# Sums of x on VectorE behind the keys, a smaller rotary table ahead of V's weights, one buffer set for key parts, output gates in the convolution's buffers

## The chip, the cores and the metric

The kernel runs on one core of one Trainium2 chip. The metric is the device time of one execution in microseconds (us). The engines are TensorE (PE, matrix products), VectorE (DVE), ScalarE (ACT), GpSimd (POOL) and the queue of SyncE (SP), which issues most transfers. Each engine works through its own list of instructions in order; an instruction whose data are not there holds everything behind it on that engine.

## The reference

One layer of a streaming encoder on 1024 prompt tokens and 64 sample tokens (1088 columns), width 1024:

```python
qa, ka, va, za, qkv_b, a_b, b_b, z_b, g_a, g_b = in_projection(x, w_in)
qa, ka = partial_rope(qa, pos), partial_rope(ka, pos)        # first 16 of 64 dims
y_a = (window_attention(qa, ka, va, sinks) * silu(za)) @ w_o_attn
qb, kb, vb = split(silu(causal_conv(qkv_b)))
y_b = (gated_rmsnorm(gated_delta_chunked(l2norm(qb), l2norm(kb), vb, g, beta)) * silu(z_b)) @ w_o_delta
h = sigmoid(g_a) * y_a + sigmoid(g_b) * y_b
y = layer_norm(ALPHA * x + h @ w_out)
```

Here g = -exp(a_log) * softplus(a_b + dt_bias) and beta = sigmoid(b_b). The partial rotary turns 16 of the 64 dimensions of each head; the other 48 stay as they are. New keys, values, convolution rows and states are outputs too.

## The kernel before, in words

All matrix products are made with operands split in a high and a low part (`split`: ACT copies the high part, DVE subtracts it to get the low part), and three products hi*hi, hi*lo, lo*hi are summed in PSUM. x lies transposed in eight tiles `ring` of 1088 columns, its raw form in `self.raw` (tiles `ring2`, shown as `ring` in the profile too).

The order of the first 165 us is: load and split x (`load_x`); project the keys for two pairs of heads in three column groups of 384, 384 and 320 (`branch_a_keys`, banks `bg`); project V and the decay inputs a, b for nine token tiles (`vab`, banks `pj`, with `wx` and `wt` as weights); project two tiles of z (`early`, banks `pj`, of which there are three), with two small groups of products of the decay (`gates`, banks `bg`) woven between; then `stream`, a Strassen-like scheme of seven products per pair of weight tiles, which needs sums and differences of blocks of x (`sums_x`) and of the weights (`weights7`).

A key group goes: ACT copies the bank to `rraw`; DVE rotates it (`rope`: a shuffle, two products with the table `cs`, an addition); ACT and DVE split it in `khi` and `klo`, of which there are two buffers each; SP writes both to DRAM (`k_d`). The sample's cached keys `ck` go the same way behind them. V's tile is evacuated by ACT (`V` at L448 and `abt` at L449). The ninth tile is added by DVE (L452). The first product of `gates` (`bg<-abt,u`) needs this `abt`; the second group (`bg<-scr,...`) needs a chain over DVE and ACT that ends with the product at L503.

```python
self.mm(sw[:, :144], swap, abt...)              # gates, after 24 products of early
nc.vector.tensor_copy(g4[...], sw[...])          # L488, L489
nc.vector.tensor_tensor(a, gbr, dtb, ALU.add)    # L495, then ACT: Abs, Exp, Ln
nc.vector.tensor_tensor(g, g, ea, ALU.mult)      # L503, then the four products
```

The sums of x are 16 subtractions of 128 x 544 values on GpSimd. They are read only from `split_sums` on, which runs with the second half of `early`.

Far later `out_a` (about 1060 to 1206 us) projects branch A's output in eight tiles; each column group is evacuated by one DVE instruction (L1134) that multiplies the bank with a gate loaded from DRAM (`gA_d`) into one of four buffers `gt`, and stored to `hA_d`. Its first tile runs while DVE works on the block inverse of branch B (L915, L917).

The code is written per stage; a list scheduler with priorities (`urgent`, `weave`) sets the order on each engine except where `keep_in_program_order` pins it. All matrix products are pinned.

Of the kernel before, what the change touches and what calls it, by code (L numbers as in the profile page):

```python
# [12 lines left out]
F32R = mybir.dt.float32r  # L13
# [3 lines left out]
ALU = mybir.AluOpType  # L17
# [7 lines left out]
NT = SEQ + DEC  # L25
# [13 lines left out]
HN = NT // 4  # L39
QUARTERS = tuple((i * HN, HN) for i in range(4))  # L40
SWAPMASK = [i + 8 if i % 16 < 8 else i - 8 for i in range(32)]
KSWAPMASK = [i + 8 if i < 8 else i - 8 if i < 16 else i for i in range(32)]
HS = (slice(0, 64), slice(64, 128))
# [12 lines left out]
class Build:  # L56
# [210 lines left out]

    def sums_x(self):
        halves = lambda k: [self.raw[k].rearrange("p (g h n) -> p h g n", g=2, h=2)[:, h] for h in range(2)]
        sub = lambda d, x, y: self.nc.gpsimd.tensor_tensor(d, x, y, ALU.subtract)  # L270
        self.late, self.mid = [], []
        with self.urgent():
            for k in range(4):
                (b11, b12), (b21, b22) = halves(k), halves(4 + k)
                t4 = self.t(self.vb, [128, 2, HN], "t4", bufs=4)
                sub(b11, b12, b11)
                t3 = self.t(self.vb, [128, 2, HN], "t3") if k == 3 else b12
                sub(t3, b22, b12)
                sub(b22, b22, b11)
                sub(t4, b21, b22)  # L280
                self.late.append(t4)
                self.mid.append(t3)
# [133 lines left out]
    def vab(self):  # L416
        nc, I = self.nc, self.I
        wt = []
        for k in (0, 4):
            wr = self.t(self.wp, [128, 4, 272], "wraw", bufs=2)  # L420
            parts = [self.t(pool, [128, 4, 272], tag, F32R, bufs=b)
                     for pool, tag, b in (((self.ws, "wx", 3), (self.ws, "wx", 3)) if k == 0 else ((self.ws, "wx", 3), (self.vb, "wt", 1)))]
            with self.urgent():
                nc.sync.dma_start(wr, I["w_vab"][k : k + 4].rearrange("k p c -> p k c"))
                self.split(*parts, wr)
            wt.append(parts)
        hi, lo = ([wt[kt // 4][s][:, kt % 4] for kt in range(KT)] for s in range(2))
        self.V = self.t(self.ap, [128, 9, 256], "V")
        abt = self.t(self.ap, [128, 9, 16], "abt")
        with self.urgent():  # L430
            rest = self.rest(self.t(self.wp, [128, KT, 128], "whi", F32R, bufs=2), self.ring)
        self.sums_x()
        nc.vector.memset(abt, 0.0)
        for t in range(9):
            m = 128 if t < 8 else 64
            ps = self.pjt()
            o = ps[:m, :272]
            for kt in range(KT):
                if t < 8:
                    xh, xl = (self.ring[kt][:, s, t * 128 : t * 128 + m] for s in (0, 1))  # L440
                    self.mm(o, xh, hi[kt], kt == 0, False)
                    self.mm(o, xl, hi[kt], False, False)
                    self.mm(o, xh, lo[kt], False, kt == KT - 1)
                else:
                    self.mm(ps[:, :272], rest[:, kt], hi[kt], kt == 0, False)
                    self.mm(ps[:, :272], rest[:, kt], lo[kt], False, kt == KT - 1)
            with self.urgent():
                nc.scalar.activation(self.V[:m, t, :], ps[:m, :256], AF.Copy)  # L448
                nc.scalar.activation(abt[:m, t, :], ps[:m, 256:272], AF.Copy)  # L449
        with self.urgent():  # L450
            for dst, c in ((self.V, slice(0, 256)), (abt, slice(256, 272))):
                nc.vector.tensor_tensor(dst[:m, 8, :], ps[64:128, c], dst[:m, 8, :], ALU.add)  # L452
        return abt
# [71 lines left out]
            nc.vector.tensor_copy(self.egs[HS[h]], self.egc[HS[1 - h]])  # L525


    def rope(self, raw, sh, a, n, swap):
        nc = self.nc
        nc.vector.stream_shuffle(sh, raw, swap)  # L530
        nc.vector.tensor_tensor(raw, raw, self.cosT[:, a : a + n], ALU.mult)
        nc.vector.tensor_tensor(sh, sh, self.sinT[:, a : a + n], ALU.mult)

    def load_rope(self, pool, name):
        cs = self.t(pool, [128, 2, NT], "cs")
# [2 lines left out]

    def branch_a_keys(self):
        nc, I = self.nc, self.I  # L540
        self.load_rope(self.vb, "rope")
        self.ck = self.t(self.vb, [128, 2, 128], "ck")
        nc.sync.dma_start(self.ck, I["cache_k"])


        def put(gp, src, dst):
            n = src.shape[-1]
            for s, part in enumerate(self.key_parts(src)):
                for hf in range(2):
                    nc.sync.dma_start(self.k_d[gp, :, 2 * s + hf, dst : dst + n], part[HS[hf]].bitcast(F32))  # L550

        for g, (a, n) in enumerate(GROUPS):
            for gp in range(2):
                ps = self.ps()[:, :n]
                for kt in range(KT):
                    self.drain(self.mm3(ps, *self.w0[gp], kt, a, n, kt == 0, kt == KT - 1))
                raw, sh = (self.t(self.vb, [128, 384], x, bufs=2)[:, :n] for x in ("rraw", "rsh"))
                nc.scalar.activation(raw, ps, AF.Copy)
                self.rope(raw, sh, a, n, KSWAPMASK)
                nc.vector.tensor_tensor(raw, raw, sh, ALU.add)  # L560
                w = min(n, SEQ - a)
                put(gp, raw[:, :w], a)
                if g == 2:
                    put(gp, raw[:, w:], SEQ + 128)
                    nc.sync.dma_start(self.O["o_nkp"][:, gp], raw[:, w - 128 : w])
                    nc.sync.dma_start(self.O["o_nks"][:, gp, 64:128], raw[:, w:])
        ck = self.ck
        for gp in range(2):
            put(gp, ck[:, gp], SEQ)
        nc.sync.dma_start(self.O["o_nks"][:, :, 0:64], ck[:, :, 64:128])  # L570

    def key_parts(self, src):
        n = src.shape[-1]
        parts = [self.t(self.vb, [128, 384], x, F32R, bufs=2)[:, :n] for x in ("khi", "klo")]
        self.split(*parts, src)
        return parts

# [9 lines left out]
    def front(self):  # L587
        nc = self.nc
        self.done = False

        def query(j):
            held = {}

            def ev(m, a, ps, add):
                g, h = divmod(a // HN, 2)
                first = (m, g) not in held
                if first:
                    held[m, g] = self.t(self.rq, [128, 2, 2 * HN], "qsp", F32R, bufs=4)
                q = held[m, g]
                parts = [q[:, s, h * HN : (h + 1) * HN] for s in range(2)]  # L600
                if j > 0 and add is None:
                    with self.urgent():
                        self.split(*parts, ps)
                else:
                    raw = self.t(self.rq, [128, HN], "rraw", bufs=4)
                    self.land(raw, ps, add)
                    if j == 0:
                        sh = self.t(self.rq, [128, HN], "rsh", bufs=2)
                        self.rope(raw, sh, a, HN, SWAPMASK)
                        nc.vector.tensor_tensor(raw, raw, sh, ALU.add)  # L610
                    self.split(*parts, raw)
                if not first:
                    for s in range(2):
                        dst = self.qd[s, 128 * j : 128 * j + 128].rearrange("p (c m i) -> p c m i", m=2, i=CH)[:, :, m]
                        w, c = q[:, s].bitcast(F32), 0 if g == 0 else 32
                        nc.sync.dma_start(dst[:, 9 * g : 9 * g + 8], w[:, c : c + 512].rearrange("p (c i) -> p c i", i=CH))
                        nc.sync.dma_start(dst[:, 8, c : c + 32], w[:, 512 - 16 * c : 544 - 16 * c])
            return ev
# [509 lines left out]
    def out_a(self, w):  # L1128
        nc = self.nc
        for t in range(8):  # L1130
            def ev(g, a, n, ps):
                tg = self.t(self.mp, [128, 384], "gt", bufs=4)
                (nc.sync if t else nc.scalar).dma_start(tg[:, :n], self.gA[t, :, a : a + n])
                nc.vector.scalar_tensor_tensor(tg[:, :n], tg[:, :n], 1.0, ps, ALU.add, ALU.mult)  # L1134
                nc.sync.dma_start(self.hA[t, :, a : a + n], tg[:, :n])
            yield from self.project(ev, edge=t in (0, 7), w=None if t else w)
# [213 lines left out]
def tables():  # L1350
# [30 lines left out]
    b = p // 16 % 2  # L1381
    masks = np.stack([f((b == 1) & (j < 16)), f((b == 0) & (j >= 16))], axis=1)
    return rope, ropeq, cf, cg, masks


# [63 lines left out]
```

## Time and profile before

| | before |
|---|---|
| median of 3 runs | 1410.66 us (1408.94 to 1410.67) |
| the profiled execution | 1408.06 us, span 1406.3 us |
| PE busy | 1364.9 us (97%) |
| DVE, ACT, POOL busy | 989.3 (70%), 624.0 (44%), 231.8 us (16%) |
| mean granted TensorE clock | 0.995 |

The span runs from the first to the last instruction; 1.8 us lie around it. Each row of a timeline has the start, the length and the instruction, then in brackets how long the engine stood idle before it and what ended the wait. A row of the waits names who waited for whom, the total, how often, and the longest.

### The profile page before, as it was taken

What the parts mean: (1) busy time and instruction counts of PE and PEld (TensorE: products, weight loads), DVE (VectorE), ACT (ScalarE), POOL (GpSimd) and SP (SyncE); (2) the same over time, 40 slices, a digit from 0 to 9 for tenths busy, and PEclk for the clock granted to TensorE, in tenths of its full rate; (3) what the DMA queues carried; (4) which work ended last, traced back from release to release, by engine and by line L of the source; (5) the groups of instructions that cost most, each with busy time, mean ns of one, the idle gap of its engine ahead of it and who ended that gap; (6) DMA issues with size and microseconds to landing.
All of it is one profiled execution on the core that took longest, in us unless ns stands there. A gap on an engine that the chain in (4) does not pass through costs nothing. (4 is left out here: it accounts for less than half of the span.)

```text
span 1406.3 us, 30878 instructions
## 1 busy us (share of the span) xinstructions
PE 1364.9 (97%) x11850; PEld 1270.8 (90%) x11850; DVE 989.3 (70%) x2404; ACT 624.0 (44%) x1764; POOL 231.8 (16%) x379
## 2 busy tenths in 40 slices
PE   8889999999999999999999999999998999999997
PEld 7889999999989899988999889988998889999886
DVE  8668555877777568867796777867788555655675
ACT  5263444555555444356633665256642443422000
POOL 4323223111111023111221113021220100000000
PEclk9999999999999999999999999999999999999998
DMA  7425566666665420210321003210346225564221
GB/s 241 117 79 131 144 135 183 190 183 180 170 183 165 123 87 31 73 36 17 93 80 57 32 24 100 82 57 17 124 137 226 73 74 167 192 219 137 95 94 71
DMA packets 152500, 162.47 MB, mean 116 GB/s; under 512 B 54304, under 2 KB 135840, under 8 KB 151968
## 3 DMA queue, kind: packets, MB, share of 16 engines
q1 hardware_dynamic: 138368, 148.59, 35.4%
q10 hardware_dynamic: 13632, 10.78, 2.5%
q8 instruction: 94, 1.54, 0.5%
q0 software_dynamic: 352, 1.11, 0.2%
q14 instruction: 54, 0.44, 0.1%
HBM read 111.74 MB, written 48.70 MB: 114 GB/s over the span
## 5 line engine op out<-in xcount | busy, mean ns | idle before, releaser
L108 PE MATMUL pj<-ring,whi 128*128 128x384 f32 (+2 forms) x2856 | 678.3, 327 | 5.8 <-DVE gt L1134 4.0
L108 PEld LDWEIGHTS pj<-ring,whi 128*128 128x128 f32 x2856 | 480.1, 189 | 17.2 <-issue 13.3
L108 PE MATMUL pj<-ring,wlo 128*128 128x384 f32 (+2 forms) x1680 | 466.2, 321 | 0.9 <-DVE rsh L471 0.8
L108 PEld LDWEIGHTS pj<-ring,wlo 128*128 128x128 f32 x1680 | 288.4, 188 | 5.8 <-issue 4.1
L812 DVE SCALAR_TENSOR_TENSOR acc<-pre,sm,acc 128x384 f32<-128x384 f32 (+1 forms) x216 | 134.0, 627 | 24.2 <-ACT acc L810 20.7
L108 PE MATMUL pj<-ring,wx 128*128 128x272 f32 x756 | 109.7, 291 | 2.9 <-ACT u L365 2.8
L88 ACT ACTIVATE whi<-wraw 128x1024 fp32r<-128x1024 f32 (+2 forms) x72 | 66.7, 927 | 82.4 <-PE pj L108 48.8
L108 PEld LDWEIGHTS pj<-ring,wx 128*128 128x128 f32 x756 | 99.6, 188 | 3.8 <-ACT u L365 3.8
L91 DVE TENSOR_TENSOR wlo<-wraw,whi 128x1024 fp32r<-128x1024 f32 (+2 forms) x58 | 68.0, 1172 | 40.4 <-ACT whi L88 35.3
L108 PE MATMUL bg<-ring,whi 128*128 128x384 f32 (+2 forms) x408 | 84.5, 317 | 5.6 <-ACT ring L88 5.2
L108 PEld LDWEIGHTS bg<-ring,whi 128*128 128x128 f32 x408 | 65.6, 190 | 7.0 <-ACT ring L88 5.2
L108 PE MATMUL pj<-pl,ring 128*128 128x512 f32 (+1 forms) x240 | 70.1, 375 | 0.0
L704 ACT ACTIVATE P<-bg,nm 128x192 f32<-128x192 f32 (+2 forms) x136 | 54.4, 408 | 33.4 <-DVE nm L697 32.1
L1024 DVE SCALAR_TENSOR_TENSOR S<-S,dec,bg 128x128 f32<-128x128 f32 x128 | 38.7, 344 | 39.2 <-PE bg L108 38.3
L813 ACT ACTIVATE gt<-acc 128x384 f32<-128x384 f32 (+1 forms) x72 | 36.4, 505 | 62.3 <-DVE acc L812 62.0
L108 PE MATMUL bg<-ring,wlo 128*128 128x272 f32 (+2 forms) x288 | 63.5, 307 | 0.0
L1002 ACT ACTIVATE qs<-bg,egs 64x128 f32<-64x128 f32 x128 | 46.4, 362 | 29.1 <-DVE R L999 27.4
L999 DVE SCALAR_TENSOR_TENSOR R<-bg,negc,t2k 64x128 f32<-64x128 f32 x128 | 44.6, 348 | 16.1 <-PE bg L108 14.9
L336 POOL TENSOR_TENSOR sums<-wraw 128x512 f32<-128x512 f32 x14 | 18.3, 1308 | 220.4 <-DMA wraw<-w_tiles 109.4
L819 DVE SCALAR_TENSOR_TENSOR plb<-gt,acc 128x384 f32<-128x384 f32 (+1 forms) x96 | 43.1, 461 | 15.6 <-ACT gt L813 15.3
L108 PEld LDWEIGHTS pj<-pl,ring 128*128 128x128 f32 x240 | 44.1, 188 | 8.2
L810 ACT ACTIVATE acc<-pre,sm 128x384 f32<-128x384 f32 (+1 forms) x72 | 42.8, 597 | 15.6 <-DVE plb L819 5.9
(277 smaller groups left out, 2317.3 us busy)
## 6 DMA issues: line engine op xcount, KB each, us to landing
wraw<-w_tiles SPq DMA_DIRECT2D x80, 512.0 KB, 3.9
q_d<-qsp SPq DMA_DIRECT2D x32, 256.0 KB, 3.5
keys<-k_d SPq DMA_DIRECT2D x28, 256.0 KB, 4.2
q<-q_d SPq DMA_DIRECT2D x64, 96.0 KB, 2.7
gA_d<-gs SPq DMA_DIRECT2D x32, 136.0 KB, 2.2
plb<-prodA SPq DMA_DIRECT2D x8, 544.0 KB, 4.4
plb<-prodB SPq DMA_DIRECT2D x8, 544.0 KB, 5.1
z<-zA_d SPq DMA_DIRECT2D x16, 256.0 KB, 3.2
```

What stands on the lines that cost most here:

```text
L88: i = self.nc.scalar.activation(hi, raw, AF.Copy)
L91: self.nc.vector.tensor_tensor(lo, raw, hi.bitcast(F32), ALU.subtract)
L108: self.tc.keep_in_program_order(self.nc.tensor.matmul(o, l, r, start=start, stop=stop, skip_group_check=skip))
L336: sub = lambda d, x, y, op: nc.gpsimd.tensor_tensor(d, x, y, op)
L704: nc.scalar.activation(P[:, hf, k], ps[:, k], AF.Exp, bias=nm[:, hf, b : b + 1], scale=0.125, accum_out=sm[:, hf, b : b + 1])
L810: nc.scalar.activation(acc[:, :w], pre[:, 0:w], AF.Copy, scale=cw(0))
L812: nc.vector.scalar_tensor_tensor(acc[:, :w], pre[:, j : j + w], cw(j), acc[:, :w], ALU.mult, ALU.add)
L813: nc.scalar.activation(th[:, :w], acc[:, :w], AF.Tanh, scale=0.5)
L819: nc.vector.scalar_tensor_tensor(o, v(th), 1.0, v(acc), ALU.add, ALU.mult)
L999: nc.vector.scalar_tensor_tensor(R[HS[h]], ks[HS[h], col[h]], self.negc[HS[h], p, c : c + 1], e["vs"][HS[h], i], ALU.mult, ALU.add)
L1002: nc.scalar.activation(qs[HS[1 - h]], ks[HS[1 - h], col[h]], AF.Copy, scale=self.egs[HS[1 - h], p, c : c + 1])
L1024: nc.vector.scalar_tensor_tensor(Sn[:, h], S[:, h], self.egl[h][:, p, c : c + 1], kv[:, 0:128], ALU.mult, ALU.add)
```

## The change

1. `sums_x` runs on VectorE instead of GpSimd, pinned in program order, and is called after the rotation of the last key group instead of ahead of V's products.
2. The rotary table of the keys is written by two memsets on GpSimd (1 and 0), and only its 2 x 16 rows that differ are loaded, ahead of V's weights, instead of the 1088 KB table behind the weights of `early`.
3. The key parts and the four sums `t4` share one set of seven buffers `parts`, instead of two `khi`, two `klo` and four `t4`. The cached keys' parts now stand behind the sums.
4. The rotation's four instructions on DVE are pinned in order, for the keys.
5. In `out_a` the gates are loaded into the convolution's buffers `acc` and `pre` (two each) and, for the third column group from tile 1 on, into `gt`.

```diff
 def sums_x(self):
-        sub = lambda d, x, y: self.nc.gpsimd.tensor_tensor(d, x, y, ALU.subtract)
+        sub = lambda d, x, y: self.tc.keep_in_program_order(self.nc.vector.tensor_tensor(d, x, y, ALU.subtract))
...
-                t4 = self.t(self.vb, [128, 2, HN], "t4", bufs=4)
+                t4 = self.t(self.vb, [128, 2 * HN], "parts", bufs=7).rearrange("p (g n) -> p g n", g=2)
 def vab(self):
-        self.sums_x()
 def rope(...):
+        keep(nc.vector.tensor_tensor(raw, raw, sh, ALU.add))
 def branch_a_keys(self):
-        self.load_rope(self.vb, "rope")
+        cs = self.t(self.vb, [128, 2, NT], "cs")
+        nc.gpsimd.memset(cs[:, 0], 1.0)
+        nc.gpsimd.memset(cs[:, 1], 0.0)
+        with self.urgent():
+            for h in HS:
+                rows = slice(h.start, h.start + 16)
+                nc.sync.dma_start(cs[rows], I["rope"][rows])
...
+        self.sums_x()
         ck = self.ck
 def key_parts(self, src):
-        parts = [self.t(self.vb, [128, 384], x, F32R, bufs=2)[:, :n] for x in ("khi", "klo")]
+        parts = [self.t(self.vb, [128, 2 * HN], "parts", F32R, bufs=7)[:, :n] for _ in range(2)]
 def out_a(self, w):
-                tg = self.t(self.mp, [128, 384], "gt", bufs=4)
+                tg = (self.t(self.mp, [128, 384], "gt", bufs=4) if t and g == 2 else
+                      self.t(self.bp, [128, (384, 390)[g % 2]], ("acc", "pre")[g % 2], bufs=2))
```

PE's order is the same in both kernels, instruction by instruction. Three places on the engines that it waits for are shown.

ACT, around the evacuation of V's last three tiles. Before, the splits of the last key group and of both halves of the cached keys (`ck`) stand between these evacuations:

```order
L448 ACTIVATE V_521<-pj_689 128x256
L449 ACTIVATE abt_522<-pj_689 128x16
L88 ACTIVATE khi_482<-rraw_467 128x64
L448 ACTIVATE V_521<-pj_716 128x256
L449 ACTIVATE abt_522<-pj_716 128x16
L88 ACTIVATE khi_492<-ck_230 128x128
L88 ACTIVATE khi_500<-ck_230 128x128
L448 ACTIVATE V_521<-pj_743 128x256
L449 ACTIVATE abt_522<-pj_743 128x16
L448 ACTIVATE V_521<-pj_770 64x256
L449 ACTIVATE abt_522<-pj_770 64x16
```

The changed kernel has at the same place (its `parts` are the former `khi`; lines count about one less here):

```order
L88 ACTIVATE parts_477<-rraw_470 128x256
L88 ACTIVATE parts_485<-rraw_470 128x64
L447 ACTIVATE V_545<-pj_719 128x256
L448 ACTIVATE abt_546<-pj_719 128x16
L447 ACTIVATE V_545<-pj_746 128x256
L448 ACTIVATE abt_546<-pj_746 128x16
L447 ACTIVATE V_545<-pj_773 64x256
L448 ACTIVATE abt_546<-pj_773 64x16
L88 ACTIVATE whi_935<-wraw_934 128x1024
L469 ACTIVATE rraw_848<-pj_800 128x384
L88 ACTIVATE parts_516<-ck_233 128x128
L88 ACTIVATE parts_524<-ck_233 128x128
```

The two splits of `ck` have moved behind the ninth tile and behind the tanh of the first z group.

DVE, between the ninth tile's addition and the chain of `gates`. Before:

```order
L452 TENSOR_TENSOR V_521<-pj_770,V_521 64x256
L452 TENSOR_TENSOR abt_522<-pj_770,abt_522 64x16
L487 COPY scr_824<-abt_522 64x9x8
L91 TENSOR_TENSOR wlo_933<-wraw_931,whi_932 128x1024
L488 COPY scr_824<-bg_822 64x9x8
L489 COPY scr_824<-bg_822 64x9x8
L471 SCALAR_TENSOR_TENSOR rraw_845<-rraw_845,pj_797 128x384
L495 TENSOR_TENSOR scr_824<-scr_824,sm_219 128x68
```

The changed kernel, from behind the same addition of `abt` on:

```order
L270 TENSOR_TENSOR ring_7_102<-ring_7_102,ring_3_98 128x2x272
L91 TENSOR_TENSOR wlo_936<-wraw_934,whi_935 128x1024
L270 TENSOR_TENSOR parts_505<-ring_7_102 128x544
L270 TENSOR_TENSOR ring_4_99<-ring_4_99 128x2x272
L270 TENSOR_TENSOR t_73_512<-ring_8_103,ring_4_99 128x544
L470 SCALAR_TENSOR_TENSOR rraw_848<-rraw_848,pj_800 128x384
L270 TENSOR_TENSOR ring_8_103<-ring_8_103,ring_4_99 128x2x272
L486 COPY scr_827<-abt_546 64x9x8
L487 COPY scr_827<-bg_825 64x9x8
L270 TENSOR_TENSOR parts_510<-ring_8_103 128x544
L91 TENSOR_TENSOR parts_517<-ck_233,parts_516 128x128
L488 COPY scr_827<-bg_825 64x9x8
```

Six of the sixteen sums (L270) stand between the addition of `abt` and the last copy out of `bg`; the other ten stand ahead of it, behind the last key's parts.

On ACT again, the stretch from the decay's exponentials to the second z group. Before, two splits of the stream's weights (`wx`) stand ahead of that group's tanh (L470):

```order
L507 ACTIVATE beta_841<-scr_824 128x68
L496 ACTIVATE scr_824<-scr_824 128x68
L497 ACTIVATE scr_824<-scr_824 128x68
L498 ACT_TABLE_LOAD
L498 ACTIVATE scr_824<-scr_824 128x68
L88 ACTIVATE wx_1080<-sums_1069 128x512
L88 ACTIVATE wx_1089<-wraw_1067 128x512
L470 ACT_TABLE_LOAD
L470 ACTIVATE rsh_889<-pj_849 128x384
```

The changed kernel:

```order
L506 ACTIVATE beta_844<-scr_827 128x68
L469 ACTIVATE rsh_892<-pj_852 128x384
L495 ACTIVATE scr_827<-scr_827 128x68
L496 ACTIVATE scr_827<-scr_827 128x68
L497 ACT_TABLE_LOAD
L497 ACTIVATE scr_827<-scr_827 128x68
L88 ACTIVATE ghi_840<-scr_827 128x68
L517 ACT_TABLE_LOAD
L517 ACTIVATE dec_882<-bg_877 128x272
```

The tanh has moved ahead of the exponentials, and the two `wx` splits have left this place; they stand some ten instructions later.

## Rows read from the trace of the kernel before

**Rows 1.** The page's busy times: us, share of the span, instructions.

```profile
PE 1364.9 (97%) x11850; PEld 1270.8 (90%) x11850; DVE 989.3 (70%) x2404; ACT 624.0 (44%) x1764; POOL 231.8 (16%) x379
```

**Rows 2.** PE's waits over the span: total us, times, longest.

```profile
PE pj L108 <- DVE gt L1134: 4.0, 1, 4.0
...
PE pj L108 <- DVE rsh L471: 2.0, 2, 1.2
...
PE pj L108 <- DVE rraw L471: 0.6, 1, 0.6
```

**Rows 3.** PE's timeline from the end of the keys to the stream.

```profile
32.38 1.92 PE L108 MATMUL pj<-wx,ring 128*128 128x272 f32 x14
...
35.38 1.93 PE L108 MATMUL pj<-wx,ring 128*128 128x272 f32 x14
...
45.36 2.33 PE L108 MATMUL pj<-wx,ring 128*128 128x272 f32 x14 [3.78 <-ACT abt L449]
...
62.62 1.30 PE L108 MATMUL pj<-wx,whi 128*128 128x272 f32 x9
...
64.62 0.51 PE L108 MATMUL pj<-ring,whi 128*128 128x384 f32 x2
...
71.30 0.48 PE L108 MATMUL bg<-abt,u 128*128 128x144 f32 x2 [2.35 <-ACT rraw L470]
...
76.45 0.44 PE L108 MATMUL bg<-scr,u 128*128 128x68 f32 x2 [0.50 <-DVE scr L503]
...
103.27 1.76 PE L108 MATMUL pj<-ring,wx 128*128 128x272 f32 x12 [0.86 <-ACT u L365]
...
117.04 1.79 PE L108 MATMUL pj<-ring,wx 128*128 128x272 f32 x12 [1.48 <-ACT u L365]
```

**Rows 4.** ACT's timeline in the stretch of V and z.

```profile
44.44 0.52 ACT L88 ACTIVATE khi<-rraw 128x384 fp32r<-128x384 f32 x1 [8.80 <-DVE rraw L560]
...
66.49 0.31 ACT L88 ACTIVATE khi<-ck 128x128 fp32r<-128x128 f32 x1 [4.03 <-DMA k_d<-khi]
...
82.90 0.63 ACT L88 ACTIVATE wx<-sums 128x512 fp32r<-128x512 f32 x1 [7.03 <-POOL sums L336]
```

**Rows 5.** DVE's timeline: rotation, decay chain, one split of 544 columns.

```profile
37.16 1.71 DVE L531 TENSOR_TENSOR rraw<-rraw,cs 128x384 f32<-128x384 f32 x1 [1.33 <-DMA cs<-rope]
...
50.87 0.55 DVE L531 TENSOR_TENSOR rraw<-rraw,cs 128x384 f32<-128x384 f32 x1
...
71.35 1.20 DVE L91 TENSOR_TENSOR wlo<-wraw,whi 128x1024 fp32r<-128x1024 f32 x1
...
72.83 0.22 DVE L489 COPY scr<-bg 64x72 f32<-64x72 f32 x1
...
76.17 0.23 DVE L503 TENSOR_TENSOR scr<-scr 128x68 f32<-128x68 f32 x1
...
101.52 0.72 DVE L91 TENSOR_TENSOR ring<-ring,ring 128x544 fp32r<-128x544 f32 x1
```

**Rows 6.** POOL's timeline: one of the sums of x.

```profile
40.05 1.67 POOL L270 TENSOR_TENSOR t<-ring,ring 128x544 f32<-128x544 f32 x1
```

**Rows 7.** SP's queue: V's weights, and the rotary table.

```profile
16.51 0.94 SPq L424 DMA_DIRECT2D wraw<-w_vab  x2
...
31.18 0.43 SPq L536 DMA_DIRECT2D cs<-rope  x1
```

**Rows 8.** Stretches: length, busy PE, PEld, DVE, ACT, POOL, clock, DMA, GB/s.

```profile
45.40:49.60 4.20, 4.20 (x24) 4.20 (x24) 4.19 (x9) 1.60 (x4) 3.73 (x9) 0.68 0.43 108
...
71.30:76.50 5.20, 4.70 (x27) 4.38 (x27) 3.51 (x10) 2.40 (x5) 0.71 (x1) 1.00 0.35 108
...
1076.70:1081.30 4.60, 4.57 (x17) 4.60 (x18) 4.53 (x7) 0.00 (x0) 0.00 (x0) 0.63 0.36 125
```

**Rows 9.** DVE's timeline where branch A's output begins.

```profile
1075.39 0.73 DVE L915 TENSOR_TENSOR t2k<-t2k,t2k 128x338 f32<-128x338 f32 x1
1076.04 1.40 DVE L1134 SCALAR_TENSOR_TENSOR gt<-gt,pj 128x384 f32<-128x384 f32 x3
```

More of the change, by code (lines that the diff above doesn't have):

```diff
@@ L525, in gates, with rope @@
             nc.vector.tensor_copy(self.egs[HS[h]], self.egc[HS[1 - h]])
-    def rope(self, raw, sh, a, n, swap):
+    def rope(self, raw, sh, a, n, swap, keep=lambda i: i):
         nc = self.nc
-        nc.vector.stream_shuffle(sh, raw, swap)
-        nc.vector.tensor_tensor(raw, raw, self.cosT[:, a : a + n], ALU.mult)
-        nc.vector.tensor_tensor(sh, sh, self.sinT[:, a : a + n], ALU.mult)
+        keep(nc.vector.stream_shuffle(sh, raw, swap))
+        keep(nc.vector.tensor_tensor(raw, raw, self.cosT[:, a : a + n], ALU.mult))
+        keep(nc.vector.tensor_tensor(sh, sh, self.sinT[:, a : a + n], ALU.mult))
+        keep(nc.vector.tensor_tensor(raw, raw, sh, ALU.add))
     def load_rope(self, pool, name):
@@ L540, in branch_a_keys @@
         nc, I = self.nc, self.I
-        self.load_rope(self.vb, "rope")
+        cs = self.t(self.vb, [128, 2, NT], "cs")
[5 more added lines that the diff above has]
+                nc.sync.dma_start(cs[rows], I["rope"][rows])
+        self.cosT, self.sinT = cs[:, 0], cs[:, 1]
         self.ck = self.t(self.vb, [128, 2, 128], "ck")
@@ L558, in branch_a_keys @@
                 nc.scalar.activation(raw, ps, AF.Copy)
-                self.rope(raw, sh, a, n, KSWAPMASK)
-                nc.vector.tensor_tensor(raw, raw, sh, ALU.add)
+                self.rope(raw, sh, a, n, KSWAPMASK, self.tc.keep_in_program_order)
                 w = min(n, SEQ - a)
@@ L609, in ev @@
                         self.rope(raw, sh, a, HN, SWAPMASK)
-                        nc.vector.tensor_tensor(raw, raw, sh, ALU.add)
                     self.split(*parts, raw)
```

## The prediction, made blind

> **What bounds the kernel now.** I read four views in this order: busy times, PE's waits, the timelines around the waits, and windows for the clock. PE is busy 1364.9 of 1406.3 us [rows 1], so some 41 us of idle PE are all that waiting can give back, and a change that leaves PE's order alone can win only there or in the clock. The waits that lie where this change works are on PE's timeline [rows 3]: 3.78 in V, 2.35 at `bg<-abt`, 0.50 at `bg<-scr`, then 0.86 and 1.48 in the stream's first products; two waits on L471's `rsh` (2.0) and one on its `rraw` (0.6) lie between these; and 4.0 far off at L1134 [rows 2]. Together 15.6 us.
>
> Follow V. Its tiles go at 35.38 - 32.38 = 3.00 us, the ninth is short, 64.62 - 62.62 = 2.00, so V needs 8 x 3.00 + 2.00 = 26.0 us; it took 64.62 - 32.38 = 32.2 [rows 3]. Of the lost 6.2, 3.78 are one wait for ACT's `abt`; after it the granted clock was 0.68 over 4.20 us [rows 8], 4.2 x 0.32 = 1.3; some 1.1 are small waits. Why is ACT late? At 44.44 it had stood 8.80 us for the rotated key [rows 4], with V's evacuations behind. DVE had begun with the table at 37.16, 1.33 late, and each 384-column product took 1.71 there and 0.55 at 50.87 [rows 5]. In the slow stretch POOL ran the sums, 1.67 each [rows 6]. So V waits for a late table and for a VectorE slowed threefold beside GpSimd. The next wait, 2.35, is ACT again: 4.03 of its time went to `khi<-ck`, which waited for the store of an older `khi` [rows 4].
>
> **The sums on VectorE, the pinned rotation, the table.** Without POOL's sums a DVE instruction on a key should cost 0.55 for 384 columns. The shuffle, which I price as the products, two products and the addition take 2.2, the high part on ACT 0.52, the low part 0.55: 3.3 a key, some 2.95 for 320 columns, by width. The table is issued ahead of V's weights, which go at 16.51 instead of the table's 31.18 [rows 7], so nothing waits for it. The first key's low part I put at 38.4, behind the `wlo` split; three more keys of 3.3 and two of 2.95 end at 54.2, and ACT never stands for long. V then ends at 32.4 + 26.0 = 58.4, 6.2 earlier. With the stall its slow clock goes.
>
> A sum has 544 columns; the DVE subtraction of 544 takes 0.72 [rows 5]. Bounds: 0.55, the 384-column price, and 1.67, POOL's price, which DVE also reached when disturbed. I take 0.72, since POOL has no sums beside it now. Sixteen are 11.5 us, which DVE had idle in V. Ten and two additions (0.8, below the two 384-column prices) stand ahead of `abt`: 54.2 + 7.2 + 0.8 = 62.2. PE takes the 24 products of z in the time it took before, 71.30 - 2.35 - 64.62 = 4.3, and is at `bg<-abt` at 62.7: no wait, where it was 71.30. That is 8.6 earlier.
>
> But six sums follow on DVE ahead of the last copy from `bg`, with one `wlo` (1.20), one L470 operation (0.5, near 0.55), a part of `ck` and two small copies (together some 0.7): 62.2 + 4.3 + 1.2 + 0.5 + 0.7 = 68.9. From the end of that copy to the end of L503 it took 76.40 - 73.05 = 3.35 [rows 5]; with 0.22 for the copy and 0.05 to PE, 3.6. `bg<-scr` starts at 72.5 and not at 76.45. PE arrives at 62.7 + (76.45 - 0.50 - 71.30 = 4.65) = 67.4 and **waits 5.1**: what the V stall was is now here, smaller by a gain of 3.95. The clock fell to 0.68 after the 3.78 wait and to 0.63 after the one at L1134, and stayed at 1.00 after 2.35 [rows 8], so it should fall again: 1.3 or 4.6 x 0.37 = 1.7, I take 1.5 (bounds 0 and 3). Net at this place -2.45.
>
> ACT's next delay goes too. It was held 7.03 at `wx<-sums` until 82.90 [rows 4] with the tanh of the second z group behind, and this is what L471 waited for; in the order shown, that tanh now stands ahead of the exponentials. So the 2.0 and 0.6 [rows 2] go, and the 0.86 and 1.48 on ACT's `u` [rows 3] as well, since ACT and the tables run several us ahead of PE: -4.9. This term is the least certain: it may be 2.6 if the `u` waits stay. Sum: -2.45 - 4.9 = **-7.35**.
>
> **Edits at nothing.** Two memsets on POOL, 1088 columns each, bounded by nothing and, twice the width of a sum, by 3.3 each; POOL's first work before was at the sums, and its end before 7 us is far ahead of the rotation. If they disturb DVE's splits of x the loss is below 1 us. [...]
>
> Two table loads of 136 KB stand ahead of V's weights in SP's queue: two issues of 0.43 [rows 7], and by bytes less than the 1088 KB one took (37.16 - 31.18 = 6 us for all, so 0.75 each). V's second tile of weights comes some 1 to 2.5 us later; it is used from 32.4 on, issued at 16.51, and has ten us of cover. [...]
>
> The shared `parts`: four stay with `t4`, three turn over for keys. I see the waits on `k_d` stores that held ACT for 4.03 move behind V, onto `ck`, whose parts nothing on PE needs soon: 0, up to 2 if `ck`'s low part ahead of the last copy waits.
>
> **out_a.** The gates get buffers earlier, but the wait of 4.0 names DVE's instruction. DVE worked on L915 until it began L1134 at 1076.04, without idle [rows 9], and that L1134 stands behind the same L915 and L917 work in both kernels. So the late thing is DVE's queue and not the gate's load: 0. With the cover gone (the load late) it could lose a us.
>
> **Total.** 1408.06 - 7.35 = 1400.7 for a profiled execution; the median of three lies 2.6 and their mean 2.0 above the profiled 1408.06, I add 2.0: 1402.7.
>
> **The rivals.**
> *A: the out_a wait goes as well.* If the gate's load, not DVE's queue, held L1134, 4.0 and the slow clock behind it (1.7) go: 1402.7 - 5.7 = 1397.0. For it: the buffers are changed there. Against: DVE's work right up to L1134. 0.10.
>
> *B: nothing measurable.* The waits move and don't shrink: `bg<-scr` waits some 3 us longer (a `ck` part that waits for a store, or sums at 0.9), the clock costs 3 instead of 1.5, and the two `u` waits (2.3) stay: 7.35 - 3 - 1.5 - 2.3 leaves 0.5, some 1409 to 1410. For it: the new chain is long and all on DVE. 0.18.
>
> *C: slower.* One mechanism: a sum costs DVE much more than 0.72. All sixteen stand ahead of the last copy, so each 0.1 is 1.6 us on `bg<-scr`; from 0.72 + 7.35 / 16 = 1.18 on the kernel is slower. At POOL's 1.67 it loses 15.2: 1402.7 + 15.2 = 1418. For it: DVE's rows beside POOL's work, and POOL still has casts and weight sums there. Against: 544 columns took 0.72 when POOL was quiet, and the two-block shape is no wider. 0.12.
>
> **How the numbers follow.** My forecast holds 0.60, with its own range of 1399 to 1406 (gains from 4 to 11: the `u` waits, the clock's bounds, sums at 0.55 to 0.85). A measurement of this kernel can tell some 0.2%, 2.8 us, from no change. Faster: 0.60 + 0.10 = 0.70, same 0.18, slower 0.12. The range must reach past A's 1397 and through most of B: 1396 to 1410.
>
> **What would show it.** V's tiles at a pace of 3.00 with no `abt` wait, its end near 58.4; 384-column key operations at 0.55 from the first one on; sums of 0.72 between 54 and 69; `bg<-scr` near 72.5 with a wait near 5 and a clock below 1 behind it; no waits on L470's evacuations (L471 before) or on `u`; the wait at out_a near 4. I am wrong if the last copy from `bg` comes later than 72.5, if the V stall remains because ACT waits for something else than the rotation, or if the waits behind `bg<-scr` stay.

## The result, and the profile after

| | before | changed |
|---|---|---|
| median (4 runs each) | 1409.80 us | 1401.92 us (1400.10 to 1402.59) |
| ratio | | 0.9942, 95% interval 0.9925 to 0.9959 |
| the profiled execution, span | 1408.06, 1406.3 | 1402.59, 1400.8 |
| mean granted TensorE clock | 0.995 | 0.993 |

The changed kernel is 0.6% faster: 7.9 us between the medians, 5.5 between the two profiled executions. The forecast of 1402.7 lies 0.8 from the median. PE's waits that answer to [rows 2] come first (total us, times, longest). Line numbers differ by a few: L502 is the former L503, L470 the former L471, L1143 the former L1134.

```profile
PE bg L108 <- DVE scr L502: 8.0, 1, 8.0
...
PE pj L108 <- DVE acc L1143: 4.0, 1, 4.0
...
PE pj L108 <- ACT u L365: 1.5, 3, 0.6
```

The waits on `abt` and on both L471 tiles are gone, those on `u` have shrunk, out_a's is what it was, and one new wait is longer than all that V lost. PE's timeline, for [rows 3]:

```profile
31.71 1.92 PE L108 MATMUL pj<-wx,ring 128*128 128x272 f32 x14
...
34.72 1.93 PE L108 MATMUL pj<-wx,ring 128*128 128x272 f32 x14
...
57.85 0.51 PE L108 MATMUL pj<-ring,whi 128*128 128x384 f32 x2
...
62.03 0.41 PE L108 MATMUL bg<-abt,u 128*128 128x144 f32 x2
...
74.62 0.69 PE L108 MATMUL bg<-scr,u 128*128 128x68 f32 x2 [8.00 <-DVE scr L502]
...
93.78 1.67 PE L108 MATMUL pj<-ring,whi 128*128 128x272 f32 x12
...
1071.22 0.98 PE L108 MATMUL pj<-ring,whi 128*128 128x384 f32 x2 [3.98 <-DVE acc L1143]
```

V runs at 3.01 a tile without a wait and ends at 57.85, not 64.62. `bg<-abt` is at 62.03, 9.3 us earlier than before. All but 1.8 of that is lost by `bg<-scr`. Why, VectorE's timeline shows (for [rows 5]), and beside it GpSimd's:

```profile
28.97 0.55 DVE L530 TENSOR_TENSOR rraw<-rraw,cs 128x384 f32<-128x384 f32 x1
...
53.85 0.72 DVE L270 TENSOR_TENSOR ring<-ring 128x544 f32<-128x544 f32 x1
...
61.64 0.17 DVE L451 TENSOR_TENSOR abt<-pj,abt 64x16 f32<-64x16 f32 x1
...
68.10 0.23 DVE L488 COPY scr<-bg 64x72 f32<-64x72 f32 x1
68.36 1.33 DVE L494 TENSOR_TENSOR scr<-scr,sm 128x68 f32<-128x68 f32 x1
...
71.88 2.42 DVE L498 SCALAR_TENSOR_TENSOR scr<-scr 128x68 f32<-128x68 f32 x1 [0.86 <-ACT scr L497]
74.33 0.23 DVE L502 TENSOR_TENSOR scr<-scr 128x68 f32<-128x68 f32 x1
```

```profile
1.71 1.00 POOL L544 MEMSET cs<- 128x1088 f32 x1
...
68.32 1.28 POOL L336 TENSOR_TENSOR sums<-wraw 128x512 f32<-128x512 f32 x1 [1.20 <-DMA wraw<-w_tiles]
...
71.72 1.27 POOL L336 TENSOR_TENSOR sums<-sums,wraw 128x512 f32<-128x512 f32 x1
72.94 1.27 POOL L336 TENSOR_TENSOR wraw<-wraw,wraw 128x512 f32<-128x512 f32 x1
```

Two instructions of 68 columns take 1.33 and 2.42 us, and each ends some 0.1 behind a GpSimd sum of the stream's weights (L336). The first was held by one sum (69.69 after 69.60). The second was held by two in a row: it began during the sum that ends at 72.99 and ended at 74.30, behind the next one's 74.21. The windows of the wait and of what follows (columns as in [rows 8]):

```profile
66.60:74.60 8.00, 0.01 (x1) 0.00 (x0) 6.90 (x13) 2.77 (x7) 4.86 (x5) 0.75 0.34 111
74.60:79.00 4.40, 4.38 (x18) 4.38 (x19) 2.12 (x7) 3.91 (x7) 0.00 (x0) 0.50 0.00 0
79.00:83.00 4.00, 4.00 (x23) 4.00 (x22) 2.98 (x6) 2.24 (x5) 0.00 (x0) 0.78 0.00 0
```

After 8.0 us without products the clock was 0.50 for 4.4 us, and 0.78 over the next four. By these windows I estimate the cost at 4.4 x 0.50 + 4.0 x 0.22 = 3.1 us.

### The profile page after: what moved, and what is told of

Its sections match the earlier page's. It is cut to its first block, busy times and chain, and to the rows that moved or that the text cites. A ratio compares the mean times of both kernels' runs of the same rounds, so it can differ in the third digit from the quotient of the medians.

```text
span 1400.8 us, 30873 instructions
## 1 busy us (share of the span) xinstructions
PE 1363.8 (97%) x11850; PEld 1271.4 (91%) x11850; DVE 984.5 (70%) x2420; ACT 625.9 (45%) x1764; POOL 206.6 (15%) x365
## 5 line engine op out<-in xcount | busy, mean ns | idle before, releaser
L336 POOL TENSOR_TENSOR sums<-wraw 128x512 f32<-128x512 f32 x14 | 18.3, 1306 | 219.0 <-DMA wraw<-w_tiles 178.9
```

The source lines that it names most:

```text
L336: sub = lambda d, x, y, op: nc.gpsimd.tensor_tensor(d, x, y, op)
```

## The experiments

| run | what | median us | ratio to before, interval |
|---|---|---|---|
| f1 | before + small table | 1409.81 | 1.0004 (0.9995 to 1.0013) |
| f2 | before + sums on VectorE, pinned rotation | 1403.19 | 0.9955 (0.9939 to 0.9970) |
| e2 | changed, sums on GpSimd | 1402.03 | 0.9940 (0.9918 to 0.9961) |
| e3 | changed, old table | 1398.71 | 0.9919 (0.9900 to 0.9938) |
| e4 | changed, old gate buffers | 1400.41 | 0.9928 (0.9910 to 0.9946) |
| g3 | changed, GpSimd quiet during the chain | 1397.35 | 0.9919 (0.9905 to 0.9932) |
| e6 | changed, unread products in the wait | 1400.19 | 0.9933 (0.9920 to 0.9946) |
| e1 | changed, half of the sums behind the chain | 1397.00 | 0.9911 (0.9896 to 0.9927) |
| e7 | changed, sums and rotation not pinned | 1397.08 | 0.9913 (0.9900 to 0.9927) |
| e5 | changed, decay products later on PE | **1395.16** | **0.9902 (0.9888 to 0.9915)** |
| g1 | e7 and e5 together | 1395.88 | 0.9909 (0.9896 to 0.9923) |

Each ratio is to the kernel before as timed beside that run (medians from 1408.9 to 1409.9); the changed kernel has 0.9942 (0.9925 to 0.9959). Of the runs that start from the changed kernel only e5 and g1 have an interval that lies wholly below its own.

**Which part freed V: f1, f2, e2, e3.** The first question is whether V's stall came from GpSimd's sums or from the late table; each was taken alone, and each taken away.

```diff
# f1, on the kernel before
-        self.load_rope(self.vb, "rope")
+        nc.gpsimd.memset(cs[:, 0], 1.0); nc.gpsimd.memset(cs[:, 1], 0.0)
+        for h in HS: nc.sync.dma_start(cs[rows], I["rope"][rows])
```

> The kernel before with the small rotary table alone (two memsets and two loads ahead of V's weights). Theory 1 (GpSimd's sums beside the rotation are V's stall, the late table only 1.3 us of it): 384-column products still 1.6 to 1.7 us, a wait of 2 to 3 on abt, 1406 to 1409. Theory 2 (the table was the stall): no wait on abt, 1400 to 1404.

Measured 1409.81, no change. PE's timeline, and VectorE's first product:

```profile
37.78 0.39 PE L108 MATMUL pj<-wt,ring 128*128 128x272 f32 x1 [2.15 <-DVE wt L91]
...
49.54 2.03 PE L108 MATMUL pj<-wx,ring 128*128 128x272 f32 x14 [1.17 <-ACT abt L449]
...
64.83 0.62 PE L108 MATMUL pj<-ring,whi 128*128 128x384 f32 x2 [0.95 <-ACT abt L449]
```

```profile
32.03 1.71 DVE L531 TENSOR_TENSOR rraw<-rraw,cs 128x384 f32<-128x384 f32 x1
```

Nothing waits for the table now, but a product still takes 1.71, and the rotation, free to start, gets ahead of the split of `wt` on VectorE: PE waits 2.15 there and twice on `abt`, 4.3 in all. Theory 1 was right about the slow products and too hopeful about the 1.3 us; the time lies 0.8 above its range.

f2 is the other half alone; table, `khi`, `klo` and `t4` stay as before.

```diff
# f2, on the kernel before; the rotation's four instructions are pinned too
-        sub = lambda d, x, y: self.nc.gpsimd.tensor_tensor(d, x, y, ALU.subtract)
+        sub = lambda d, x, y: keep(self.nc.vector.tensor_tensor(d, x, y, ALU.subtract))
...
-        self.sums_x()        # in vab
+        self.sums_x()        # in branch_a_keys, behind the last rotation
```

> The kernel before with the sums of x on VectorE behind the last key, and the pinned rotation, alone (full table late in SP's queue, two khi, two klo and four t4 buffers). Theory 1 (GpSimd's sums made the table late too, since the table's issue waits for a buffer that VectorE frees): the table issued near 26 instead of 31, no wait on abt in V, a wait at the decay's products of 3 to 8 as in the changed kernel, 1398 to 1404. Theory 2 (the table must be ahead as well): a wait of 2 or more on abt stays, 1404 to 1408.

```profile
23.27 1.29 DVE L91 TENSOR_TENSOR wx<-wraw,wx 128x1088 fp32r<-128x1088 f32 x1 [1.38 <-ACT wx L88]
...
31.26 0.56 DVE L530 TENSOR_TENSOR rraw<-rraw,cs 128x384 f32<-128x384 f32 x1 [4.47 <-DMA cs<-rope]
```

```profile
24.59 0.33 SPq L146 DMA_DIRECT2D wraw<-w_tiles  x1
24.97 0.55 SPq L536 DMA_DIRECT2D cs<-rope  x1
```

```profile
76.52 0.70 PE L108 MATMUL bg<-scr,u 128*128 128x68 f32 x2 [7.15 <-DVE scr L502]
```

Measured 1403.19. The full table goes out at 24.97 and not at 31.18 [rows 7], though its place in SP's queue is the same: the load ahead of it is issued at 24.59, when VectorE's split has read V's weights out of that buffer (23.27 + 1.29 = 24.56). In the kernel before, the same split on VectorE and the same load in SP's queue are:

```profile
28.83 1.95 DVE L91 TENSOR_TENSOR wx<-wraw,wx 128x1088 fp32r<-128x1088 f32 x1
...
30.81 0.33 SPq L146 DMA_DIRECT2D wraw<-w_tiles  x1
```

There the split ends at 30.78 and the load follows at 30.81, with the table behind it. So the late table was an effect of the slow VectorE. V has no wait on `abt`. One of 1.9 stands at `bg<-abt`, until the ninth tile has been added, and the wait at `bg<-scr` is there, 7.2. Theory 1 held. The sums on VectorE with the pinned rotation make 6.0 of the 7.9 us (the kernel before took 1409.19 beside this run). That V runs free does not hang on the pinned order: in e7, without it, V does not wait either.

```diff
# e2, on the changed kernel (called ahead of V's products again)
-        sub = lambda d, x, y: keep(self.nc.vector.tensor_tensor(...))
+        sub = lambda d, x, y: self.nc.gpsimd.tensor_tensor(...)
# e3, on the changed kernel: f1 the other way round
```

> The changed kernel with the sums of x on GpSimd again, called ahead of V's products as before; table, parts, pinned rotation and gate buffers stay changed. Theory 1 (GpSimd's sums slow VectorE threefold and so starve V): rotation at 1.6 to 1.7 us an instruction again until about 45 us, a wait of 2 to 4 on abt in V with a slow clock behind it, 1404 to 1408. Theory 2 (the late table was the cause of V's stall): no wait in V, and the wait at the decay's products gone, 1393 to 1398.

Measured 1402.03, as fast as the changed kernel, with GpSimd's timeline so:

```profile
37.94 1.56 POOL L270 TENSOR_TENSOR ring<-ring,ring 128x544 f32<-128x544 f32 x1
...
64.97 6.11 POOL L270 TENSOR_TENSOR parts<-ring 128x544 f32<-128x544 f32 x4 [20.84 <-DMA k_d<-parts]
```

Neither theory as I put it. V does not stall, but not because of the table: the four sums that write `parts` now wait for buffers until 64.97, so GpSimd is done with the other twelve at 39.5 and not past 45, and the pinned rotation's products run at 0.55 to 0.65 from 42 on. In exchange the stream's waits stay (2.7 and 1.6 on `u`, 0.8 and 0.2 on L471), and there are 1.4 and 2.0 at the two decay products. The parts of the change are not additive: here the wait for the shared buffers kept four of GpSimd's sums away from the rotation. What the pinned order added to that, no run takes apart.

> The changed kernel with the full rotary table loaded as before. Theory 1 (the table was a small part; VectorE has slack before the first key): the rotation starts near 37 instead of 28, the keys end 2 to 3 us later, V does not wait, and the wait at the decay's products grows by as much: 1403.5 to 1405.5. Theory 2 (the table is half of V's stall): a wait of 2 to 4 on abt in V comes back, 1405 to 1408.

Measured 1398.71, which neither theory allowed: 3.2 below the changed kernel, though the two intervals overlap. V has no wait; the keys end at 53.3, no later, since in the changed kernel VectorE stood 5.68 anyway, ahead of the `wlo` split and the first key's low part. PE comes to `bg<-abt` 2 us later (64.03), and of the small instructions one falls ahead of GpSimd's sum from 69.73 to 70.99 and the other, begun at 70.25, beside the end of that sum alone (0.29 and 0.82 instead of 1.33 and 2.42): the wait at `bg<-scr` is 2.8. The slow clock comes with this shorter wait too: 0.89 over 60 to 90, an estimated 30 x 0.11 = 3.3 us. So no gain of the small table shows here, and how long the new wait is hangs on where GpSimd's sums fall. That became the next question.

**What the new wait is made of: g3, e6.**

```diff
# g3: in weights7, first call only; gf is the chain's result
+            nc.gpsimd.tensor_copy(S[:, 0, 0, :68], self.gf)
             sub(s1, a21, a22, ALU.add)
```

> The changed kernel with GpSimd's first sums of the stream's weights held until the decay chain has ended (a copy of 68 columns of its result into their tile, overwritten afterwards). Theory 1 (three of the eight us of the wait are VectorE's small instructions slowed by those sums): the chain's instructions 0.2 to 0.3 us each, from the last copy to the decay's products 3.5 to 4 us instead of 6.5, the wait 5 to 6, 1398.5 to 1400.5. Theory 2 (the small instructions wait for something else): they stay at 1.3 and 2.4, 1401.5 or more.

```profile
68.33 0.22 DVE L491 COPY scr<-bg 64x72 f32<-64x72 f32 x1
68.58 0.27 DVE L497 TENSOR_TENSOR scr<-scr,sm 128x68 f32<-128x68 f32 x1
...
71.33 0.23 DVE L501 SCALAR_TENSOR_TENSOR scr<-scr 128x68 f32<-128x68 f32 x1 [0.97 <-ACT scr L500]
```

```profile
71.87 0.69 PE L108 MATMUL bg<-scr,u 128*128 128x68 f32 x2 [5.05 <-DVE scr L505]
```

From the copy to the products 71.87 - 68.33 = 3.5 us, as the prediction had it, and the wait is 5.05, its 5.1. Measured 1397.35, 1.2 below what theory 1 gave. That the sums of the weights slowed the chain is shown. The clock behind the wait is as slow as before:

```profile
74.00:79.00 5.00, 5.00 (x21) 5.00 (x21) 4.48 (x9) 3.64 (x7) 0.00 (x0) 0.54 0.00 0
```

It is 0.54 over these 5 us. PE's pace shows the price. From `bg<-scr` to the stream's first product it needs 90.38 - 74.11 = 16.3 us in the profile of e6 (below), with a clock of 1.00; here it took 91.30 - 71.87 = 19.4, in the changed kernel 93.78 - 74.62 = 19.2, in f2 95.09 - 76.52 = 18.6, and in e3, from the end of the chain, 90.81 - 71.40 = 19.4. So the slow clock cost 2.9 us behind the changed kernel's wait of 8.0 (3.1 by the windows), 2.3 behind f2's 7.2, and 3.1 to 3.2 behind 5.05 here and behind e3's 2.8, each in one profile. In these four a shorter wait gave back its own length and nothing of the clock.

```diff
# e6: in gates, ahead of the four decay products
+        for i in range(65):
+            self.mm(ps[:, 272:512], self.ring[i % 8][:, 0, :128], self.ring[i % 8][:, 0, 128:368], True, True, True)
```

> The changed kernel with 65 products of 240 columns, never read, on PE ahead of the decay's products (about 7 us of work inside the wait of 8.0). Theory 1 (some 3 us of the time are the slow clock behind the idle stretch): granted clock 1.00 from 67 to 83, the time 2 to 3.5 us shorter than the changed kernel, 1398 to 1400. Theory 2 (the slow clock is not due to PE's idleness there, or hides nothing): 1401.5 or more.

```profile
66.83 7.44 PE L108 MATMUL bg<-ring 128*128 128x240 f32 x65
...
74.11 0.34 PE L108 MATMUL bg<-scr,u 128*128 128x68 f32 x2
```

```profile
60.00:90.00 30.00, 30.00 (x208) 29.90 (x207) 26.58 (x47) 16.56 (x33) 8.37 (x9) 1.00 0.28 86
```

The profiled execution did as theory 1 says: clock 1.00 and 1397.2 us, with more work on PE. In it the chain, little hindered by GpSimd's sums, had ended at 72.14, so the unread products even held the decay's products back by 2 us. The other runs go up to 1402.5, and the median of 1400.19 does not stand clear of the changed kernel's. That the clock stays up with products in the wait, 1.00 over 60 to 90 and not the changed kernel's 0.83, is seen in the profile; what that is worth in time is not settled by this run.

**Taking the wait away: e1, e7, e5, g1.** e1 splits the call of the sums.

```diff
# e1
-        self.sums_x()
+        self.sums_x((0, 1))
...
-        nc.vector.tensor_tensor(g, g, ea..., ALU.mult)
+        keep(nc.vector.tensor_tensor(g, g, ea..., ALU.mult))   # L502
+        self.sums_x((2, 3))
```

> The changed kernel with only the first eight sums ahead of the decay chain on VectorE and the other eight behind it. Theory 1 (the eight-us wait at the decay's products is VectorE's queue of sums plus its clock): the wait falls to 0 to 2 us, the slow clock behind it goes, and the time is 1391 to 1394. Theory 2 (the late sums are what the stream needs, so the wait only moves): new waits on the splits of the sums or on z's banks take over half back, 1397 to 1401.

```profile
90.30 1.67 PE L108 MATMUL pj<-ring,wx 128*128 128x272 f32 x9 [0.80 <-ACT u L364]
...
94.02 0.60 PE L108 MATMUL pj<-ring,wx 128*128 128x272 f32 x1 [2.04 <-ACT ring L88]
```

The wait is gone, and half comes back some 25 us later: the stream waits for the splits of the late sums, with a clock of 0.89 over 90 to 120. Measured 1397.00: theory 2.

```diff
# e7
-        sub = lambda d, x, y: keep(self.nc.vector.tensor_tensor(d, x, y, ALU.subtract))
+        sub = lambda d, x, y: self.nc.vector.tensor_tensor(d, x, y, ALU.subtract)
-                self.rope(raw, sh, a, n, KSWAPMASK, keep)
+                self.rope(raw, sh, a, n, KSWAPMASK)
```

> The changed kernel without the pinned order of the sums and of the rotation on VectorE: eleven of the sixteen sums then stand between the last split of x and the first rotation, where VectorE is idle in the changed kernel (some 8 us near 21 to 30). Theory 1 (the wait at the decay's products is those sums in front of its chain): the wait falls to 0 to 2, no slow clock, 1390 to 1395. Theory 2 (the early sums hold V's weight splits, L91 on wx and wt): a new wait of 1 to 4 near 32 us, 1394 to 1400.

```profile
69.31 0.44 PE L108 MATMUL bg<-scr,u 128*128 128x68 f32 x2 [1.53 <-DVE scr L502]
...
106.50 1.79 PE L108 MATMUL pj<-ring,wx 128*128 128x272 f32 x12 [1.05 <-ACT u L365]
...
132.19 1.77 PE L108 MATMUL bg<-ring,wx 128*128 128x272 f32 x12 [1.58 <-ACT u L365]
```

Twelve sums ran between 19.9 and 30.2 on VectorE, where it had stood idle for some 4 us in the changed kernel; V's weights were in time. The wait is 1.53. Measured 1397.08: theory 1's wait, but not its time. The clock still fell, to 0.94 over 60 to 90: from `bg<-scr` to the stream PE took 87.21 - 69.31 = 17.9 us, 1.6 more than in e6's profile, and in the stream 1.05 and 1.58 on `u` stay.

```diff
# e5, in gates and plain
-        yield 24 * 384
+        yield 24 * (384 + 320 + 384)
...
-            for _ in range(8):
+            for _ in range(4):
                 next(work, None)
```

> The changed kernel with the four decay products moved on PE behind 56 more z products (three groups later instead of one), the sums' splits woven in closer. Theory 1 (the wait at the decay's products and its slow clock cost 8 + 3 us, and z's products can fill it as the unread ones did): no wait there, granted clock 1.00 from 67 to 83, 1390 to 1394. Theory 2 (the later decay or the closer splits hold z's banks or the stream): the waits come back there, 1396 to 1401.

```profile
74.19 0.33 PE L108 MATMUL bg<-scr,u 128*128 128x68 f32 x2
...
91.36 0.52 PE L108 MATMUL pj<-ring,wx 128*128 128x272 f32 x2 [1.28 <-DVE ring L91]
...
93.92 0.39 PE L108 MATMUL pj<-ring,wx 128*128 128x272 f32 x1 [2.04 <-ACT ring L88]
...
95.56 0.82 PE L108 MATMUL pj<-ring,wx 128*128 128x272 f32 x2 [1.25 <-DVE ring L91]
```

```profile
90.00:120.00 30.00, 25.43 (x188) 24.93 (x188) 26.27 (x64) 14.22 (x30) 6.56 (x4) 0.94 0.34 100
```

There is no wait at the decay's products, the clock is 1.00 up to 90, and the time is 1395.16: 6.8 us below the changed kernel by the medians, 5.9 when each is set against the kernel before as timed beside it. It is the lowest median here, got by filling the wait and not by shortening the chain; the intervals of e1, e7, g1 and others overlap its own. It misses theory 1's 1394: the stream now begins 11.0 us earlier (82.78 instead of 93.78) and meets the splits of the sums, with 4.6 us of new waits and a clock of 0.94 over 90 to 120 (an estimated 30 x 0.06 = 1.8 us). The run has two edits, the later products and the closer splits; they were not taken apart.

> Both edits at once: sums and rotation without a pinned order (early sums in VectorE's idle stretch) and the decay's products three groups later on PE. Theory 1 (each alone leaves a small rest, 1.5 us of wait in the one, late sums for the stream in the other): 1389 to 1393, the fastest of all. Theory 2 (what remains are the waits on u in the stream, whatever stands ahead): as the better of the two alone, 1393 to 1397.

Measured 1395.88, no better than e5: theory 2. The stream still waits 2.0 for a split and 2.9 on `u`.

**The gates' buffers in out_a: e4.**

```diff
# e4
-                tg = (gt if t and g == 2 else acc or pre)
+                tg = self.t(self.mp, [128, 384], "gt", bufs=4)
```

> The changed kernel with out_a's gates in four gt buffers as before. Theory 1 (the wait of 4.0 at branch A's first tile is VectorE's queue, not the gate's load): the time of the changed kernel within 1 us, the wait 4.0 in both. Theory 2 (the buffers took away later waits in out_a): 1 to 3 us slower, with waits on the gate tiles.

Measured 1400.41, with a wait of 4.1. That is 1.5 below the changed kernel, more than theory 1's 1 us, but its interval covers most of the changed kernel's, and the wait is for VectorE's instruction in both. The gate buffers do nothing that can be measured.

## Why the prediction was right, point by point

- **V's stall.** The prediction was right that it goes: V took 57.85 - 31.71 = 26.1 us instead of 32.2, at 3.01 a tile and without a wait. f2 shows it with the sums on VectorE and the old table. The step that named the late table as a second cause was wrong: f1 and f2 show that the small table is neither sufficient nor needed. One reading was wrong without effect on the time: VectorE stood idle for 8.0 us in V before (busy 24.27 of 32.24), not for 11.5.
- **VectorE's prices.** They were right: 0.55 for a product, and 0.72 a sum from 53.85 on. The keys ended at 53.9 (54.2 forecast), `abt` at 61.8 (62.2), and `bg<-abt` started at 62.03 (62.7).
- **The new wait.** Place and cause were right, the size too small: 8.0 instead of 5.1. The last copy ended at 68.33 (68.9 forecast). The mis-sized term is the chain behind it: 3.6, from a stretch in which GpSimd was quiet. It took 74.62 - 68.10 = 6.5, and 3.5 with GpSimd held back (g3). The rival C had GpSimd's weight sums in view, for the sums of x; they met the small instructions instead.
- **The clock.** The forecast was 1.5, with bounds 0 and 3; the windows give 3.1, just past the upper bound, and PE's pace 2.9.
- **ACT's delays behind.** The forecast was -4.9. The waits on L471 and the two on `u` that were named are gone, but three of 0.48, 1.00 and 0.55 on `u` stand at other places, where none was forecast. From `bg<-scr` to the next common point, a wait at 279.93 before and 274.74 now, PE gained (279.93 - 76.45) - (274.74 - 74.62) = 3.4 in spite of the 3.1 of slow clock: some 6.5. Of this 4.5 are the listed waits (6.5 before, 2.0 after); the rest was not traced.
- **Sum.** -1.83 + 3.1 - 6.5 = -5.2 at that point, where -7.35 was forecast; it is 5.5 between the profiled executions (1402.59, where 1400.7 was forecast). That the medians came out 0.8 apart owes something to luck: the profiled run of before is faster than its four timed ones, that of the changed kernel the slowest of its four, so the 2.0 us added for the median made up for the missing gain.
- **Edits at nothing.** This was right. The two memsets took 1.0 us each and were done at 2.7, ahead of VectorE's first split at 3.6, so what they do to a split was not seen. V's weights were issued 0.8 us later (17.27) and were late for nobody; out_a's wait is 3.98 after 3.97. What GpSimd's sums do to VectorE was seen later: the two 68-column instructions, 0.27 and 0.23 us alone, ended some 0.1 behind GpSimd's sums of 1.28 and 1.27 us.

## What to carry to other kernels

Work moved from one engine to another should be placed by what stands behind it in the new engine's queue: here a chain of tiny instructions stood behind six of the large ones, and PE waited for it. Price such a chain by a stretch in which the neighbour engine is as busy as it will be: 3.6 became 6.5. Where a wait can't be taken away whole, move independent products into it. That kept the clock up as well (1.00 over 60 to 90 in e6 and e5), while waits cut to 5.05 or 2.8 us still had some 3 us of slow clock behind them. It gave the lowest median here, 1395.2 against 1397.0 for the best reordering of VectorE, but the intervals of the two overlap.

## What was not expected of the hardware

VectorE's small instructions suffered most from GpSimd, where 384 columns went from 0.55 to 1.71: 68 columns took 0.23 to 0.29 us alone and 1.33, 2.42 and, in f2's profile, 2.83 beside its sums, the last two behind two sums in a row. And a transfer can be late because of an engine that has no part in it: the table left at 31.18 or at 24.97 by nothing but the speed of VectorE's splits, through a buffer that the load ahead of it in the queue needed.
